# Second eight heads: products for the softmax maxima on half of the array's rows each, in pairs, with one maximum over two banks

## The chip, the core and the metric

The kernel runs on one core of a Trainium2 chip. The metric is the device time of one execution in microseconds (us). Engines are named as in the profile: PE is TensorE's matmul, PEld its loading of stationary operands ("weights"), DVE is VectorE, ACT ScalarE, POOL GpSimd, SP SyncE, which here only issues transfers (DMA).

## What is computed

One layer of attention with two kinds of heads, and one gated layer behind it. The change is in the attention of the second kind, `q_b`, `k_b`, `v_b`: eight query heads of width 64, four of which share one head of keys and values, 2048 queries, and 256 + 2048 keys.

```python
def block_attention(q, k, v, scale):
    ...
    def one_block(qi):
        sc = jnp.einsum('bqhgd,bthd->bhgqt', qi, k).astype(jnp.float32) * scale
        p = jax.nn.softmax(sc, axis=-1).astype(v.dtype)
        return jnp.einsum('bhgqt,bthe->bqhge', p, v)
    ...
o_a = block_attention(q_a[:, :, :, None], k_a, v_a, A_SCALE)        # 8 heads of width 96
o_b = block_attention(q_b.reshape(bsz, n, B_KV_HEADS, B_GROUP, B_HD), k_b, v_b, B_SCALE)   # 8 heads of width 64
```

Queries and keys are held as two fp32r numbers each, a rounded value (h) and the rest (l), so that a product of two such operands takes several matmuls.

## The kernel before, in words

`phase1` projects the input and leaves queries, keys and values in HBM. `attention` works through 64 **items**, one for each head and each quarter of the queries (512 of them): items 0 to 31 belong to the first eight heads, items 32 to 63 to the second. `phase3` is the output projection and the second layer.

An item has 18 **steps**, one for every 128 keys (`score`, then `low`, `add`, `mul`):

- `score`: PE makes the scores of 128 keys and 512 queries in PSUM (tile `s`, 3 buffers). In the second heads that is two matmuls: one over 128 rows (64 rows hold h, 64 rows l), and one over 65 rows, of which the last is a row of ones against the negative maximum of each query. ACT takes the exponential twice, once rounded (`ph`) and once in full, back into `s`.
- `low`: DVE subtracts the two and leaves `pl`. For two of the 18 steps POOL does this (the tuple `shares(i)[0]`), with a copy into `ph` first.
- `add`: POOL sums `ph` over the keys, for 12 of the 18 steps; for the other six PE adds them up with one matmul more (`ol<-ph,last`), and at the end with two (`sh`, `sl`).
- `mul`: four steps or more later PE multiplies `ph` and `pl` with the values (`oh`, `ol`).

The maxima must be there before an item's first score. Ten steps ahead (`AHEAD`) of it, and spread over 18 steps, `peak` has PE multiply queries and keys without their low halves into a tile `m` of one PSUM bank, two of which take turns (`peak_products`, L603 and L607), and `top` has DVE take the maximum over the keys (`peak_maxima`, L617 and L620): 16 times over 512 keys, and twice over 2 x 256 keys (two matmuls of 256 columns). At the last of them DVE takes the maximum of the 20 partial ones, negated (`nm`, L623), SP stores it to HBM (`NM<-nm`, L624), and `peak_row` loads it as a row of the query tile (`q<-NM`, L537), on which the 65-row matmul of the item's first step waits. [...]

The order on each of PE, DVE, ACT and POOL is written out: `at(time, unit)` gives each unit of work a time in steps, the units are sorted by it, and `InOrder` holds each engine to that order (its call is L588, hence one line for nearly all instructions of the attention). `queries` loads an item's query tile (3 buffers), `keys` the keys and values of a head (2 buffers); in the second heads a load of 64 rows each.

Of the kernel before, what the change touches and what calls it, by code (L numbers as in the profile page):

```python
# [12 lines left out]
F32 = mybir.dt.float32  # L13
F32R = mybir.dt.float32r
AF = mybir.ActivationFunctionType
ALU = mybir.AluOpType
AX = mybir.AxisListType
PSUM = bass.MemoryType.PSUM

P = 128  # L20
# [3 lines left out]
CTX = 256  # L24
NT = SEQ + CTX
NTT = NT // P
CH = 512
EPS = 1e-6
NH = 8
QR, KVR = 384, 256  # L30
NOPE, ROPE, DV = 64, 32, 64
HD = 64
# [36 lines left out]
def phase1(e):  # L69
    nc, tc, I = e.nc, e.tc, e.ins  # L70
    early = ExitStack()
    with tc.tile_pool(name="p1c", bufs=1) as cp, tc.tile_pool(name="p1", bufs=2, reuse_waits="tile") as sp, \
# [207 lines left out]
        for half in range(2):  # L280
# [197 lines left out]
            if half == 1:  # L478
                e.first = keys(e, 0), [queries(e, 0, g) for g in range(2)]
                todo = first_peaks(e, sp, pp)  # L480
# [55 lines left out]
def load(e, dst, src):  # L536
    e.nc.sync.dma_start(dst.bitcast(F32), src)  # L537


def keys(e, h):  # L540


    nc = e.nc
    K = e.kp.tile([P, 2, NT], F32R, name="k", tag="k", bufs=2)
    V = e.kp.tile([P, NTT, 2 * DV + 2], F32R, name="v", tag="v", bufs=2)
    if h < NH:
        load(e, K[:NOPE], e.KA[:, h * NOPE:(h + 1) * NOPE, :].rearrange("s p t -> p s t"))
        load(e, K[NOPE:NOPE + ROPE], e.KR.rearrange("s p t -> p s t"))
        nc.gpsimd.memset(K[NOPE + ROPE:NOPE + ROPE + 1, 0, :].bitcast(F32), 1.0)
        load(e, V[:, :, :2 * DV], e.VA[h])  # L550
    else:
        g = (h - NH) // 4
        load(e, K[:HD], e.KB[:, g * HD:(g + 1) * HD, :].rearrange("s p t -> p s t"))
        load(e, K[HD:, 0, :], e.KB[0, g * HD:(g + 1) * HD, :])
        nc.gpsimd.memset(K[HD:HD + 1, 1, :].bitcast(F32), 1.0)
        load(e, V[:, :, :2 * DV], e.VB[g])
    nc.gpsimd.memset(V[:, :, 2 * DV:2 * DV + 1].bitcast(F32), 1.0)
    return K, V


def queries(e, h, g):

    cs = slice(g * CH, (g + 1) * CH)
    Q = e.kp.tile([P, 2, CH], F32R, name="q", tag="q", bufs=3)
    if h < NH:
        load(e, Q[:NOPE], e.QN[:, h * NOPE:(h + 1) * NOPE, cs].rearrange("s p t -> p s t"))
        load(e, Q[NOPE:NOPE + ROPE], e.QP[:, h * ROPE:(h + 1) * ROPE, cs].rearrange("s p t -> p s t"))
    else:
        j = h - NH
        for i in range(2):  # L570
            load(e, Q[i * HD:(i + 1) * HD, 0, :], e.QB[i, j * HD:(j + 1) * HD, cs])
        load(e, Q[:HD, 1, :], e.QB[0, j * HD:(j + 1) * HD, cs])
    return Q


# [1 line left out]
AHEAD = 10  # L577
# [19 lines left out]
def peak_products(e, PE, pp, pms, at, i, K, Q, m, tag="m", bufs=2):  # L597

    r = NOPE + ROPE if at[0] < NH else P
    pm = pms[i, m] = pp.tile([P, CH], F32, name="m", tag=tag, bufs=bufs)  # L600
    if m < 16:
        j, c = divmod(m, 4)
        PE.matmul(pm, lhsT=Q[:r, 0, j * P:(j + 1) * P], rhs=K[:r, 0, c * CH:(c + 1) * CH], start=True, stop=True)  # L603
    else:
        for u in range(2):
            j = 2 * (m - 16) + u
            PE.matmul(pm[:, u * CTX:(u + 1) * CTX], lhsT=Q[:r, 0, j * P:(j + 1) * P], rhs=K[:r, 0, 4 * CH:],  # L607
                      start=True, stop=True)


def peak_maxima(e, DVE, sp, pms, stats, i, m):

    if m == 0:
        stats[i] = sp.tile([P, 4, 5], F32, name="mx", tag="mx", bufs=2)
    pm = pms.pop((i, m))
    if m < 16:
        DVE.tensor_reduce(out=stats[i][:, m // 4, m % 4:m % 4 + 1], in_=pm, axis=AX.X, op=ALU.max)  # L617
    else:
        j = 2 * (m - 16)
        DVE.tensor_reduce(out=stats[i][:, j:j + 2, 4], in_=pm.rearrange("p (j k) -> p j k", j=2), axis=AX.X, op=ALU.max)  # L620
    if m == 17:
        nm = sp.tile([P, 4], F32R, name="nm", tag="nm", bufs=2)
        DVE.tensor_reduce(out=nm, in_=stats.pop(i), axis=AX.X, op=ALU.max, negate=True)  # L623
        e.nc.sync.dma_start(e.NM[i:i + 1, :].rearrange("o (j p) -> p (o j)", p=P), nm.bitcast(F32))  # L624


def peak_row(e, h, i, Q):

    dst = Q[NOPE + ROPE:NOPE + ROPE + 1, 0, :] if h < NH else Q[HD:HD + 1, 1, :]
    load(e, dst, e.NM[i:i + 1, :])  # L630


def first_peaks(e, sp, pp):

    nc, (K, _), Q = e.nc, e.first[0], e.first[1]
    e.stats, pms = {}, {}

    def one(i, m):
        peak_products(e, nc.tensor, pp, pms, (0, i), i, K, Q[i], m, "misc", 3)
        peak_maxima(e, nc.vector, e.kp, pms, e.stats, i, m)  # L640

    return [lambda i=i, m=m: one(i, m) for i, n in ((0, NTT), (1, AHEAD)) for m in range(n)]


def attention(e):
# [3 lines left out]
    nc, tc = e.nc, e.tc  # L649
    PE, DVE, ACT, POOL = (InOrder(tc, x) for x in (nc.tensor, nc.vector, nc.scalar, nc.gpsimd))  # L650
# [3 lines left out]
    with tc.tile_pool(name="atc", bufs=1, reuse_waits="tile") as cp, \  # L654
            tc.tile_pool(name="at", bufs=2, reuse_waits="tile") as sp, \
            tc.tile_pool(name="atps", bufs=1, space=PSUM, reuse_waits="tile") as pp:
        NG = SEQ // CH
        work = [(h, g) for h in range(2 * NH) for g in range(NG)]
        NW = len(work)
        kv, qs, stats, pms, pts = {}, {}, {}, {}, {}  # L660
        acc, tot, gates, outs = {}, {}, {}, {}
        kv[0], (qs[0], qs[1]) = e.first

        last = cp.tile([P, DV + 2], F32R, name="last")
# [3 lines left out]
        def shares(i):  # L668

            if i >= NW - NG:  # L670
                return (), ()
            if i < NH * NG:
                return (4,), tuple(t for t in range(17) if t != 4)
            return (2, 8), tuple(t for t in range(16) if t not in (2, 5, 8, 12))

        def fetch_keys(h):
            kv[h] = keys(e, h) if h < NH or h % 4 == 0 else kv[h - 1]

        def fetch_queries(i):
            qs[i] = queries(e, *work[i])  # L680

        def peak(i, m):
            peak_products(e, PE, pp, pms, work[i], i, kv[work[i][0]][0], qs[i], m)

        def top(i, m):
            peak_maxima(e, DVE, sp, pms, stats, i, m)

        def row(i):
            peak_row(e, work[i][0], i, qs[i])

        def score(s):

            i, t = divmod(s, NTT)
            h, g = work[i]
            K, Q = kv[h][0], qs[i]
            ks = slice(t * P, (t + 1) * P)
            ps = pp.tile([P, CH], F32, name="s", tag="s", bufs=3)
            m = NOPE + ROPE
            if h < NH:
                prods = [(K[:m + 1, 0, ks], Q[:m + 1, 0, :]), (K[:m, 1, ks], Q[:m, 0, :]), (K[:m, 0, ks], Q[:m, 1, :])]  # L700
            else:
                prods = [(K[:, 0, ks], Q[:, 0, :]), (K[:HD + 1, 1, ks], Q[:HD + 1, 1, :])]
            for u, (a, b) in enumerate(prods):
                PE.matmul(ps, lhsT=a, rhs=b, start=u == 0, stop=u == len(prods) - 1)

            ph = sp.tile([P, CH], F32R, name="ph", tag="ph", bufs=LAGP + 3)
            pl = sp.tile([P, CH], F32R, name="pl", tag="pl", bufs=LAGP + 3)
            if t in shares(i)[0]:
                ps, pf = sp.tile([P, CH], F32, name="pf", tag="pf", bufs=2), ps
                ACT.activation(ps, pf, AF.Exp)  # L710
            else:
                ACT.activation(ph, ps, AF.Exp)
                ACT.activation(ps, ps, AF.Exp)
            pts[s] = (ph, pl, ps)
# [75 lines left out]
        def at(time, *unit):  # L790
            units.append((time, len(units), unit))

        stats.update(e.stats)
        for i in range(NW):
            if i > 1:
                at((i - 2) * NTT + 1.2, fetch_queries, i)
            if i % NG == 1 and i // NG + 1 < 2 * NH:
                at(i * NTT + 1.2, fetch_keys, i // NG + 1)
            for m in range((NTT, AHEAD)[i] if i < 2 else 0, NTT):
                at(i * NTT - NTT - AHEAD + m + 0.6, peak, i, m)  # L800
                at(i * NTT - NTT - AHEAD + m + 1.3, top, i, m)
            at(max(0, i * NTT - AHEAD + 2.5) - (i == 0), row, i)
        for s in range(NW * NTT):
            i, t = divmod(s, NTT)
            parts, adds = shares(i)
            at(s, score, s)
            at(s + (0.9 if t in parts else 1.6), low, s)
            if t in adds:
                at(s + 1.0, add, s)
            if adds and t == adds[-1]:  # L810
                at(s + 1.1, total, i)
            place = s + (LAGP if t in parts else LAG + (LATE[t] if t < len(LATE) else 0))
            at(place + 0.7, mul, s)
            if t == NTT - 1:
                at(place + 0.9, take, i)
                at(place + 2.3, finish, i)
# [16 lines left out]
            at(end - (NG - 1) * NTT + 4 * k + 17, lambda k: z_split(e, e.Z[0][k], sp.tile([P, CH], F32, name="zt", tag="zt", bufs=2), POOL), k)  # L833
        for _, _, (f, *args) in sorted(units):
            f(*args)


def phase3(e):
# [356 lines left out]
```

## Time and profile before

| | |
|---|---|
| time, median of 3 runs (range) | 3336.63 us (3332.5 to 3338.37) |
| the profiled execution: its own time, its span | 3341.19 us, 3339.4 us |
[...]
| PE, DVE, ACT, POOL busy, share of the span | 96%, 76%, 57%, 53% |
| scores of the first heads, and of the second | from 686.0 to 1536.34 us, and from there to 2319.4 us |

The attention is read from stretches of the span, not from the shares of the whole: in it DVE and POOL are far busier than the means say. A matmul's end is modelled, and a matmul of 512 columns is shown with 0.39 to 0.40 us although the next one starts 0.23 us later; so PE's pace is read from the starts of successive matmuls, and a wait from a start that comes late. The same holds for DVE, whose instructions overlap by some 0.08 us.

### The profile page before, as it was taken

To read this page: it belongs to the slowest core of one execution; us is meant where nothing else is said; L and a number is where in the kernel's file an instruction comes from. 1 tells how busy PE (TensorE), PEld (TensorE's weight loads), DVE (VectorE), ACT (ScalarE), POOL (GpSimd) and SP (SyncE) were. 2 spreads that over 40 slices of the span, in tenths; PEclk is the share of its full clock that TensorE was granted. 3 is DMA by queue.
4 is the path that set the end of the run, shared out by engine and by line. 5 is a ranking of instruction groups with operands and counts; after the bars stand their busy time and mean duration, and the time that the engine had idled before them with its cause. 6 is when DMAs were issued, how large, how long until landed. Compare 5 with 4: busy or idle time off the path is not lost.

```text
span 3339.4 us, 40476 instructions
## 1 busy us (share of the span) xinstructions
PE 3200.2 (96%) x13698; PEld 2435.2 (73%) x13698; DVE 2541.0 (76%) x3621; ACT 1890.9 (57%) x3258; POOL 1777.9 (53%) x1423
## 2 busy tenths in 40 slices
PE   7999999989999999999999999999899999899998
PEld 3886777767777777777666666677688788688786
DVE  4847794578988889888999999996745755755746
ACT  3433342257777777777777777776343353353342
POOL 3312431269999999998888888854301301301201
PEclk9999999989999999999999999999999999999999
DMA  6446745552122231222111111113533533533322
GB/s 231 141 163 188 231 146 188 159 124 62 39 49 60 60 65 39 49 60 60 30 28 30 28 43 33 28 29 61 158 94 108 151 95 110 146 97 108 107 89 76
DMA packets 187057, 314.09 MB, mean 94 GB/s; under 512 B 53264, under 2 KB 79184, under 8 KB 184928
## 3 DMA queue, kind: packets, MB, share of 16 engines
q1 hardware_dynamic: 178558, 283.62, 30.2%
q0 software_dynamic: 8000, 27.81, 2.8%
q8 instruction: 108, 1.77, 0.3%
q14 instruction: 101, 0.83, 0.1%
q10 hardware_dynamic: 290, 0.07, 0.0%
HBM read 240.71 MB, written 70.73 MB: 93 GB/s over the span
## 4 chain that ended last, share of the span: by engine, by line
PE 52%; DMA 10%; POOL 8%; DVE 8%; issue 5%; ACT 3%; SPq 0%; POOLq 0%; ACTq 0%; DVEq 0%
PE s L588 12%; POOL sa L588 6%; PE ol L588 6%; DMA NM<-nm 6%; PE oh L588 4%; PE m L588 4%; PE acc L1011 4%; PE acc L1010 4%; PE acc L1009 4%; PE acc L915 3%; PE acc L914 3%; PE acc L916 3%; DVE pl L588 2%; DMA q<-NM 2%; DMA w<-in_o_w_in 1%
## 5 line engine op out<-in xcount | busy, mean ns | idle before, releaser
L588 POOL TENSOR_TENSOR sa<-sa,ph 128x512 f32<-128x512 f32 x728 | 939.7, 1291 | 61.0 <-ACT ph L588 15.5
L588 PE MATMUL s<-q,k 96*128 96x512 f32 (+2 forms) x2880 | 874.3, 400 | 40.8 <-DVE pl L588 22.9
L588 DVE TENSOR_TENSOR pl<-s,ph 128x512 fp32r<-128x512 f32 x1064 | 728.6, 685 | 115.7 <-ACT s L588 93.0
L588 ACT ACTIVATE ph<-s 128x512 fp32r<-128x512 f32 x1064 | 633.7, 596 | 310.8 <-PE s L588 294.1
L588 DVE TENSOR_REDUCE mx<-m 128x1 f32<-128x512 f32 x1124 | 763.7, 682 | 58.7 <-PE m L588 55.2
L588 PEld LDWEIGHTS s<-q,k 96*128 96x128 f32 (+2 forms) x2880 | 538.9, 190 | 253.3 <-DVE pl L588 45.5
L588 ACT ACTIVATE s<-s 128x512 f32<-128x512 f32 x1064 | 632.7, 595 | 0.0
L588 PE MATMUL oh<-ph,v 128*128 128x512 f32 x1152 | 455.5, 395 | 0.0
L588 PE MATMUL ol<-pl,v 128*65 128x512 f32 x1152 | 455.1, 395 | 0.0
L588 PE MATMUL m<-k,q 128*128 128x512 f32 (+1 forms) x1250 | 451.2, 377 | 0.0
L65 ACT ACTIVATE wh<-w 128x1024 fp32r<-128x1024 f32 x153 | 162.2, 1060 | 491.3 <-PE acc L916 219.2
L66 DVE TENSOR_TENSOR wl<-w,wh 128x1024 fp32r<-128x1024 f32 x153 | 202.2, 1321 | 267.6 <-ACT wh L65 266.8
L1020 POOL TENSOR_TENSOR u<-u,y 128x512 f32<-128x512 f32 x32 | 63.6, 1988 | 416.7 <-ACT y L1019 416.7
L588 PEld LDWEIGHTS m<-k,q 128*128 128x128 f32 (+1 forms) x1250 | 234.7, 190 | 67.2 <-DVE mx L588 14.3
L177 PE MATMUL ps<-xl,wh 128*128 128x512 f32 (+1 forms) x640 | 250.3, 391 | 6.9 <-DVE xl L168 6.8
L176 PE MATMUL ps<-xh,wh 128*128 128x512 f32 (+1 forms) x640 | 249.1, 390 | 6.3 <-POOL wh L147 3.4
L588 PEld LDWEIGHTS oh<-ph,v 128*128 128x128 f32 x1152 | 217.9, 189 | 49.5
L178 PE MATMUL ps<-xh,wl 128*128 128x512 f32 (+1 forms) x640 | 248.8, 389 | 1.7 <-DVE wl L148 1.7
L588 PEld LDWEIGHTS ol<-pl,v 128*65 128x65 f32 x1152 | 157.4, 137 | 50.7 <-ACT ob L588 0.3
L914 PE MATMUL acc<-wh,k 128*128 128x512 f32 x384 | 159.7, 416 | 24.1 <-DVE y L1046 18.6
L915 PE MATMUL acc<-wl,k 128*128 128x512 f32 x384 | 158.4, 412 | 8.5 <-DVE wl L66 8.4
L916 PE MATMUL acc<-wh,k 128*128 128x512 f32 x384 | 156.9, 409 | 0.0
(300 smaller groups left out, 5372.5 us busy)
## 6 DMA issues: line engine op xcount, KB each, us to landing
w<-in_wug SPq DMA_DIRECT2D x64, 512.0 KB
wr<-in_w SPq DMA_DIRECT2D x38, 512.0 KB
w<-in_e_w_out SPq DMA_DIRECT2D x32, 512.0 KB
w<-in_o_w_in SPq DMA_DIRECT2D x32, 512.0 KB
w<-in_o_w_out SPq DMA_DIRECT2D x32, 512.0 KB
wr<-in_e_w_mod SPq DMA_DIRECT2D x24, 512.0 KB
wr<-in_o_w_mod SPq DMA_DIRECT2D x24, 512.0 KB
q<-QB SPq DMA_DIRECT2D x96, 128.0 KB
```

Of the source, the lines that this page charges most:

```text
L65: e.nc.scalar.activation(h, src, AF.Copy)
L66: e.nc.vector.tensor_tensor(out=l, in0=src, in1=h.bitcast(F32), op=ALU.subtract)
L176: nc.tensor.matmul(out, lhsT=wh(k), rhs=xh(k), start=i == 0, stop=False)
L177: nc.tensor.matmul(out, lhsT=wh(k), rhs=xl(k), start=False, stop=False)
L178: nc.tensor.matmul(out, lhsT=wl(k), rhs=xh(k), start=False, stop=i == n - 1)
L588: i = getattr(self.engine, name)(*args, **kw)
L914: nc.tensor.matmul(ps[t], lhsT=h[:, ts], rhs=w[0][:, k, :], start=first, stop=False)
L915: nc.tensor.matmul(ps[t], lhsT=h[:, ts], rhs=w[1][:, k, :], start=False, stop=False)
L916: nc.tensor.matmul(ps[t], lhsT=l[:, ts], rhs=w[0][:, k, :], start=False, stop=last)
L1009: nc.tensor.matmul(ps, lhsT=w[0][:, k, :], rhs=h, start=k == 0, stop=False)
L1010: nc.tensor.matmul(ps, lhsT=w[0][:, k, :], rhs=l, start=False, stop=False)
L1011: nc.tensor.matmul(ps, lhsT=w[1][:, k, :], rhs=h, start=False, stop=k == NK - 1)
```

## The change

For the second heads alone, products for the maxima are made in pairs. The keys' high halves, which lay in rows 0 to 63 of the key tile, now lie there and in rows 64 to 127, and so do the queries'. A product contracts over 64 rows; one of a pair uses rows 0 to 63, the next one rows 64 to 127, and they write two neighbouring banks of one tile `m` of two banks, of which there is one buffer (before: two buffers of one bank). The pair is made at every second step. One maximum instruction takes both banks: 8 with 2 x 512 keys, and one with 4 x 256. The pool of `m` is closed and opened anew at item 32, where the form of the tile changes.

The scores' second matmul has 128 rows in place of 65: rows 0 to 63 are now ones in row 0 against the negative maximum, and zeros, which POOL sets once for each head of keys. A query tile is loaded with four transfers of 64 rows in place of three. The first heads, the scores themselves, exponentials, sums and products with the values are as before.

```diff
@@ keys @@
     else:
         g = (h - NH) // 4
-        load(e, K[:HD], e.KB[:, g * HD:(g + 1) * HD, :].rearrange("s p t -> p s t"))
-        load(e, K[HD:, 0, :], e.KB[0, g * HD:(g + 1) * HD, :])
-        nc.gpsimd.memset(K[HD:HD + 1, 1, :].bitcast(F32), 1.0)
+        load(e, K[HD:], e.KB[:, g * HD:(g + 1) * HD, :].rearrange("s p t -> p s t"))
+        load(e, K[:HD, 0, :], e.KB[0, g * HD:(g + 1) * HD, :])
+        nc.gpsimd.memset(K[:HD, 1, :].bitcast(F32), 0.0)
+        nc.gpsimd.memset(K[:1, 1, :].bitcast(F32), 1.0)
         load(e, V[:, :, :2 * DV], e.VB[g])
@@ queries @@
         for i in range(2):
             load(e, Q[i * HD:(i + 1) * HD, 0, :], e.QB[i, j * HD:(j + 1) * HD, cs])
-        load(e, Q[:HD, 1, :], e.QB[0, j * HD:(j + 1) * HD, cs])
+
+        for i in range(2):
+            load(e, Q[i * HD:(i + 1) * HD, 1, :], e.QB[0, j * HD:(j + 1) * HD, cs])
@@ new @@
+def pair_products(PE, pm, K, Q, m):
+
+    parts = [(Q[:HD, 0], K[:HD, 0]), (Q[HD:, 1], K[HD:, 0])]
+    for u in range(1 if m < 8 else 2):
+        for v, (q, k) in enumerate(parts):
+            if m < 8:
+                j, c = divmod(2 * m + v, 4)
+                PE.matmul(pm[:, v], lhsT=q[:, j * P:(j + 1) * P], rhs=k[:, c * CH:(c + 1) * CH], start=True, stop=True)
+            else:
+                j = 2 * v + u
+                PE.matmul(pm[:, v, u * CTX:(u + 1) * CTX], lhsT=q[:, j * P:(j + 1) * P], rhs=k[:, 4 * CH:], start=True, stop=True)
+
+
+def pair_maxima(e, DVE, sp, pm, stats, i, m):
+
+    if m == 0:
+        stats[i] = sp.tile([P, 4, 5], F32, name="mx", tag="mx", bufs=2)
+    if m < 8:
+        j, c = divmod(2 * m, 4)
+        DVE.tensor_reduce(out=stats[i][:, j, c:c + 2], in_=pm, axis=AX.X, op=ALU.max)
+    else:
+        DVE.tensor_reduce(out=stats[i][:, :, 4], in_=pm.rearrange("p v (u k) -> p (v u) k", u=2), axis=AX.X, op=ALU.max)
+        stored(e, DVE, sp, stats, i)
@@ peak_row @@
-    dst = Q[NOPE + ROPE:NOPE + ROPE + 1, 0, :] if h < NH else Q[HD:HD + 1, 1, :]
+    dst = Q[NOPE + ROPE:NOPE + ROPE + 1, 0, :] if h < NH else Q[:1, 1, :]
@@ attention @@
         def peak(i, m):
-            peak_products(e, PE, pp, pms, work[i], i, kv[work[i][0]][0], qs[i], m)
+            if i < NH * NG:
+                peak_products(e, PE, mp[0], pms, work[i], i, kv[work[i][0]][0], qs[i], m)
+            elif m % 2:
+                pms[i] = mp[0].tile([P, 2, CH], F32, name="m", tag="m", bufs=1)
+                pair_products(PE, pms[i], kv[work[i][0]][0], qs[i], m // 2)
 
         def top(i, m):
-            peak_maxima(e, DVE, sp, pms, stats, i, m)
+            if i < NH * NG:
+                peak_maxima(e, DVE, sp, pms, stats, i, m)
+            elif m % 2:
+                pair_maxima(e, DVE, sp, pms.pop(i), stats, i, m // 2)
...
-                prods = [(K[:, 0, ks], Q[:, 0, :]), (K[:HD + 1, 1, ks], Q[:HD + 1, 1, :])]
+                prods = [(K[:, 0, ks], Q[:, 0, :]), (K[:, 1, ks], Q[:, 1, :])]
```

`stored` holds the three lines that made `nm` and its store, word for word; they follow the ninth maximum now.

PE in the steady part of the second heads, before: in a row of four steps or so, where `s` are the scores, `m` the products for the maxima, `oh` and `ol` those with the values.

```order
L588 MATMUL m<-k,q 128x512
L588 MATMUL oh<-ph,v 128x512
L588 MATMUL ol<-pl,v 65x512
L588 MATMUL s<-q,k 128x512 x2
L588 MATMUL m<-k,q 128x512
L588 MATMUL oh<-ph,v 128x512
L588 MATMUL ol<-pl,v 65x512
```

The same place after the change:

```order
L591 MATMUL m<-k,q 128x512 x2
L591 MATMUL oh<-ph,v 128x512
L591 MATMUL ol<-pl,v 65x512
L591 MATMUL s<-q,k 128x512 x2
L591 MATMUL oh<-ph,v 128x512
L591 MATMUL ol<-pl,v 65x512
L591 MATMUL s<-q,k 128x512 x2
L591 MATMUL m<-k,q 128x512 x2
```

Two products `m` stand side by side at every second step where one stood at each; the full-height matmuls between two such places are six (or seven, with an `ol<-ph,last`).

DVE in the same part, before: maxima (`mx`) and subtractions (`pl`) alternate, and `nm` closes an item's maxima.

```order
L588 TENSOR_REDUCE mx<-m 128x2
L588 TENSOR_TENSOR pl<-s,ph 128x512
L588 TENSOR_REDUCE mx<-m 128x2
L588 TENSOR_REDUCE nm<-mx 128x4
L588 TENSOR_TENSOR pl<-s,ph 128x512
L588 TENSOR_REDUCE mx<-m 128x1 x2
L588 TENSOR_TENSOR pl<-s,ph 128x512
L588 TENSOR_REDUCE mx<-m 128x1
L588 TENSOR_TENSOR pl<-s,ph 128x512
```

The same place after the change:

```order
L591 TENSOR_TENSOR pl<-s,ph 128x512 x2
L591 TENSOR_REDUCE mx<-m 128x4
L591 TENSOR_REDUCE nm<-mx 128x4
L591 TENSOR_TENSOR pl<-s,ph 128x512
L591 TENSOR_REDUCE mx<-m 128x2
L591 TENSOR_TENSOR pl<-s,ph 128x512 x2
L591 TENSOR_REDUCE mx<-m 128x2
L591 TENSOR_TENSOR pl<-s,ph 128x512 x2
```

A maximum now stands between two pairs of subtractions, and `nm` follows a single maximum of four columns instead of two of two.

## Rows read from the trace of the kernel before

**Rows 1.** Busy time by stretch: length, PE, PEld, DVE, ACT, POOL, PEclk, DMA, GB/s.
```profile
1497.00:1523.00 26.00, 26.00 (x115) 20.08 (x114) 23.38 (x39) 19.90 (x37) 23.70 (x20) 1.00 0.10 25
1601.00:2211.00 610.00, 593.44 (x2502) 420.99 (x2503) 565.16 (x928) 479.75 (x900) 509.83 (x426) 1.00 0.13 31
```
**Rows 2.** Timeline of SP's issues: start, us, engine, line, operation, tiles.
```profile
1601.32 0.39 SPq L624 DMA_DIRECT2D NM<-nm  x1
...
1992.18 0.39 SPq L624 DMA_DIRECT2D NM<-nm  x1
2000.91 0.22 SPq L537 DMA_DIRECT2D q<-NM  x1
2003.20 1.73 SPq L537 DMA_DIRECT2D q<-QB  x3
```
**Rows 3.** Timeline of PE, a run of eight matmuls without a wait, second heads.
```profile
2021.98 0.39 PE L588 MATMUL m<-k,q 128*128 128x512 f32 x1
...
2023.85 0.62 PE L588 MATMUL s<-q,k 128*128 128x512 f32 x2
```
**Rows 4.** Timeline of PE where it waits; in brackets, idle time and what ended it.
```profile
2004.43 0.50 PE L588 MATMUL s<-q,k 65*128 65x512 f32 x1 [0.32 <-DMA q<-NM]
...
2012.22 0.40 PE L588 MATMUL m<-k,q 128*128 128x256 f32 x2
2012.46 0.39 PE L588 MATMUL oh<-ph,v 128*128 128x512 f32 x1
2012.69 0.40 PE L588 MATMUL ol<-pl,v 128*65 128x512 f32 x1
2013.56 0.73 PE L588 MATMUL s<-q,k 128*128 128x512 f32 x2 [0.48 <-DVE pl L588]
2014.16 0.51 PE L588 MATMUL m<-k,q 128*128 128x256 f32 x2
2014.51 0.39 PE L588 MATMUL oh<-ph,v 128*128 128x512 f32 x1
```
**Rows 5.** Groups of 1601 to 2211 us: count, busy us, mean ns, idle before.
```profile
L588 DVE TENSOR_REDUCE mx<-m 128x1 f32<-128x512 f32 (+1 forms) x451 | 305.4, 682 | 21.9 <-PE m L588 21.2
L588 PE MATMUL s<-q,k 128*128 128x512 f32 (+1 forms) x902 | 294.7, 404 | 16.6 <-DVE pl L588 12.3 <-DMA q<-NM 3.4
```
**Rows 6.** Timeline of DVE, second heads, without a wait.
```profile
2011.38 1.40 DVE L588 TENSOR_TENSOR ob<-oh,ob 64x512 f32<-64x512 f32 x2
...
2016.53 0.17 DVE L588 TENSOR_REDUCE nm<-mx 128x4 fp32r<-128x20 f32 x1
...
2017.22 1.28 DVE L588 TENSOR_REDUCE mx<-m 128x1 f32<-128x512 f32 x2
```
**Rows 7.** Timeline of POOL at the same place.
```profile
2016.71 0.62 POOL L588 TENSOR_SCALAR ph<-pf 128x512 fp32r<-128x512 f32 x1
...
2018.66 4.03 POOL L588 TENSOR_TENSOR sa<-sa,ph 128x512 f32<-128x512 f32 x3
```
**Rows 8.** Timeline of PE where matmuls of 2 columns (L118, L273) meet full ones.
```profile
17.79 7.03 PE L118 MATMUL ps<-wr,sc 128*2 128x512 f32 x16
...
534.91 0.39 PE L178 MATMUL ps<-xh,wl 128*128 128x512 f32 x1
535.23 3.59 PE L273 MATMUL rows<-acc,pick 128*2 128x512 f32 x8
538.75 0.51 PE L176 MATMUL ps<-wh,ch 128*128 128x512 f32 x1
539.10 0.40 PE L177 MATMUL ps<-wl,ch 128*128 128x512 f32 x1
```
**Rows 9.** Timeline of PE where matmuls of 64 columns (L418) meet full ones.
```profile
556.97 0.39 PE L418 MATMUL ps<-xl,wh 128*64 128x512 f32 x1
557.20 0.39 PE L176 MATMUL ps<-xh,wh 128*128 128x512 f32 x1
557.42 0.39 PE L177 MATMUL ps<-xl,wh 128*128 128x512 f32 x1
```

More of the change, by code (lines that the diff above doesn't have):

```diff
@@ L608, in peak_products, with stored @@
                       start=True, stop=True)
+def pair_products(PE, pm, K, Q, m):
[17 more added lines that the diff above has]
+        stored(e, DVE, sp, stats, i)
+def stored(e, DVE, sp, stats, i):
+    nm = sp.tile([P, 4], F32R, name="nm", tag="nm", bufs=2)
+    DVE.tensor_reduce(out=nm, in_=stats.pop(i), axis=AX.X, op=ALU.max, negate=True)
+    e.nc.sync.dma_start(e.NM[i:i + 1, :].rearrange("o (j p) -> p (o j)", p=P), nm.bitcast(F32))
 def peak_maxima(e, DVE, sp, pms, stats, i, m):
@@ L621, in peak_maxima @@
     if m == 17:
-        nm = sp.tile([P, 4], F32R, name="nm", tag="nm", bufs=2)
-        DVE.tensor_reduce(out=nm, in_=stats.pop(i), axis=AX.X, op=ALU.max, negate=True)
-        e.nc.sync.dma_start(e.NM[i:i + 1, :].rearrange("o (j p) -> p (o j)", p=P), nm.bitcast(F32))
+        stored(e, DVE, sp, stats, i)
 def peak_row(e, h, i, Q):
-    dst = Q[NOPE + ROPE:NOPE + ROPE + 1, 0, :] if h < NH else Q[HD:HD + 1, 1, :]
+    dst = Q[NOPE + ROPE:NOPE + ROPE + 1, 0, :] if h < NH else Q[:1, 1, :]
     load(e, dst, e.NM[i:i + 1, :])
@@ L661, in attention, with banks @@
         acc, tot, gates, outs = {}, {}, {}, {}
+        mpool, mp = ExitStack(), []
+        def banks(k):
+            mpool.close()
+            mp[:] = [mpool.enter_context(tc.tile_pool(name="mps%d" % k, bufs=1, space=PSUM, reuse_waits="tile"))]
+        banks(0)
         kv[0], (qs[0], qs[1]) = e.first
@@ L798, in attention @@
                 at(i * NTT + 1.2, fetch_keys, i // NG + 1)
+            if i == NH * NG:
+                at(i * NTT - NTT - AHEAD + 0.6, banks, 1)
             for m in range((NTT, AHEAD)[i] if i < 2 else 0, NTT):
@@ L835, in attention @@
             f(*args)
+        mpool.close()
 def phase3(e):
```

## The prediction

> **What bounds the kernel now.** I first ask which engine sets the pace of the second heads, since only there anything changes. The length of an item comes from SP's issues: the store of the maxima `NM<-nm` returns once per item, and from 1601.32 to 1992.18 us it returns 16 times [rows 2], so an item takes 24.43 us. What PE needs for it comes from a run without a wait: from 2021.98 to 2023.85 us eight matmuls start, one every 0.234 us [rows 3]. By the code an item has 36 of them for scores, 18 + 18 with the values, 8 that sum `ph`, and 16 of 512 columns plus 4 of 256 for the maxima. That is 96 x 0.234 = 22.5 us, and the four short ones take 0.24 us for one pair (2012.22 to 2012.46) and 0.35 for the other (2014.16 to 2014.51) [rows 4]: 23.1 us together. So PE is occupied for 23.1 of 24.43 us and waits for about 1.4 us per item. The reader sees where: at the first step for the row of maxima (`q<-NM`, 0.32 us), some nine microseconds later for `pl` (0.48 us) [rows 4], in sum 12.3 us for `pl` and 3.4 for the row over 25 items [rows 5]; the rest is small change around these.
>
> The other engines are close behind. DVE starts an instruction of 512 columns every 0.60 us (two in 1.28 us, the last 0.68 long) [rows 5, 6]; 16 subtractions and 18 maxima are 20.4 us, two `ob` 1.4 and `nm` 0.1: 21.9 us. POOL has 15 operations at 4.03 / 3 = 1.34 us and two copies of 0.62 [rows 7]: 21.3 us. In the first heads, where PE's need is larger (three matmuls per score), it has no gap at all, 26.00 busy of 26.00 us, with DVE and POOL at 90% [rows 1]. So whatever PE gains in the second heads meets POOL and DVE after some two microseconds, and whatever it loses is paid almost in full, less the part of the 1.4 us of waits that goes away.
>
> **The change, part by part.**
>
> *Maxima on DVE.* 682 ns for 512 columns and 174 for the 20 of `nm` [rows 5, 6] give 1.03 ns per column, so 1024 columns end 0.53 us later: 1.13 us from start to start. Nine of them are 10.2 us against 18 x 0.60 = 10.8. DVE needs 21.3 us instead of 21.9, a saving of 0.6 us on an engine that isn't the bound; it can only shorten the waits for `pl`. Against this stands that `nm` comes 0.53 us later behind its last product.
>
> *Products side by side.* Two products took 0.468 us of PE's stream. If both halves of the array run at once, a pair takes 0.234. No row of before shows two matmuls at once; the bounds are 0.234 and 0.468. I take 0.234: the two share no row of the array and no PSUM bank, and PE does overlap what shares nothing (in [rows 3] each matmul's weights are loaded under the one before, or eight could not start every 0.234 us). [...]
>
> *Going to the half array and back.* This is the term that decides. The trace has a place where PE leaves the full array for a small part of it and returns: eight matmuls with 2 columns of weights among full ones [rows 8]. Sixteen such matmuls take 7.03 us and eight take 3.59, so one takes 0.43. The first one starts 0.32 us after the full matmul in front, not 0.234: 0.09 us to go there. Eight take 3.52 us to the start of the next full one, not 3.44: 0.08 to 0.09 back. And the second full one starts 0.35 us after the first, not 0.234: 0.11, since its predecessor's weights weren't loaded ahead. The other such place speaks against a price: matmuls with 64 columns of weights pass into full ones at 0.23 and 0.22 us [rows 9]. Which of the two is the pair like? Those with 2 columns leave most of the array unused as the halves do, and run in fp32; those with 64 columns are fp32r, as the products here are. I go by [rows 8], since the halves have to run side by side to be of use, so the array really must be divided, and nothing in [rows 9] gains from a division. [...]
>
> The pair is then 0.09 in + 0.11 for weights that can't be loaded ahead + 0.234 for both + 0.09 out + 0.11 for the next full weights = 0.63 us, and 0.74 if the second half's weights queue behind the first's. Against 0.468 that is +0.17 to +0.28; I take +0.22, eight times per item: +1.8. The ninth group, four matmuls of 256 columns, took 0.59 and takes 0.09 + 0.11 + two rounds of 0.12 + 0.09 + 0.11 = 0.64, up to 0.97 with three more unhidden loads: +0.05 to +0.4, taken as +0.2. PE's need rises by 2.0 us per item (1.4 to 2.6), to 25.1.
>
> *What comes back.* With 25.1 us of its own PE runs against DVE's and POOL's 21.3, nearly the relation of the first heads, where it waits for nothing. The wait for `pl` stands behind the two `ob` (1.40 us of DVE at once [rows 6]) and should halve, as the step grows longer and DVE's share of it shorter. The wait for `q<-NM` stays: from the store's issue at 1992.18 to the first score that uses it at 2004.43 is 12.25 us [rows 2, 4]; `nm` comes 0.53 us later, and ten steps of PE's longer pace give about as much back. I take 0.5 us off the 1.4 (0.1 to 1.0).
>
> *The rest.* The fourth load of queries adds an issue of 1.73 / 3 = 0.58 us on SP [rows 2], behind `q<-NM` and seven steps ahead of its use; queued behind it is the store of the previous item, for which nobody waits. The second matmul of a score has 128 rows in place of 65 and the same 512 columns, which set its time: nothing. Zeros on POOL: twice in all. The single tile `m` of two banks makes PE wait for the maximum two steps (2.7 us) earlier; 0.4 + 1.13 us and a subtraction of 0.60 in front fit. Where the `ob` fall in between, 1.4 us more don't quite: up to 0.5 us per item, inside my upper bound.
>
> Sum: +2.0 - 0.5 = +1.5 us per item, for 32 items +48 us (0.4 to 2.5 per item: +13 to +80). On the profiled execution's 3341.19 us that is 3389; it lies 4.6 us above the median of the runs, so the forecast for the median is 3385 (3350 to 3417).
>
> **Rivals.**
>
> *The change to half the array is free*, as in [rows 9]. Then PE saves 8 x 0.234 + 0.3 = 2.2 us and needs 20.9, and POOL's and DVE's 21.3 become the bound. But the ring over HBM also stands: 12.25 us from store to score, plus 0.53, plus the 11.6 us from there to the next store (24.43 - 12.25, less some 0.6 of waits), now at 21.3 / 23.1 of their length: 23.5 us. So 0.9 us less per item at the least, 2.5 at the most (21.3 and a wait of 0.6); taken as 1.2, -38 us: 3299 (3257 to 3308). It decides as soon as both crossings and their loads cost under 0.234 us together. For it: [rows 9], the same number type. Against: [rows 8]. [...]
>
> *The two halves run one after the other*, so the change doesn't do what it says. A pair is 0.09 + 0.11 + 0.468 + 0.09 + 0.11 = 0.87 us, +0.40; with +0.4 for the ninth group +3.6 per item. Waits give back 0.8: +2.8, +90 us, 3427 (3405 to 3455). Speaking for it: no row shows an overlap of matmuls.
>
> *Waits swallow the price.* Crossings fall where PE would have waited for DVE anyway and nearly all of the 1.4 us goes away: +0.0 to +0.2 per item, 3330 to 3343. Against it: pairs stand at fixed steps, waits at two or three of 18.
>
> **How the numbers follow.** Forecast 0.55, one after the other 0.17, free 0.20, swallowed 0.08. The likeliest is 3385. The range takes in all but the free case and the far end of the serial one: 3330 to 3440. A measurement of this kernel tells about 0.2% (7 us) from no change; so slower 0.72, same 0.07 and faster 0.21, which is the free case and the swallowed one's edge.
>
> **What would show it.** In the profile after: the item's length from the `NM<-nm` issues, 25.9 us if right, 23.2 if the change is free, 27.2 if serial. Around a pair on PE, from the last full matmul's start to the first full one's after the pair: 0.76 to 0.87 us in place of 0.70 (0.47 if free, 0.99 if serial), the two products' starts at most 0.11 apart, and the second full matmul behind a pair 0.34 us after the first. Weight loads behind a pair that start with their matmul, not ahead. Maxima of 1.2 us. I am wrong if the pair's products start 0.23 apart, or if full weights are loaded while a pair runs.

## The result, and the profile after

The change made the kernel slower: 3358.7 us (3356.24 to 3361.63) against 3337.5 us for the kernel before, a ratio of 1.0063 [1.0045, 1.0082]. The forecast was 3385 with a range of 3330 to 3440: the direction and the range hold, but the loss is 21 us where 48 were forecast.

The busy times from the head of the profile page of after, and its chain of work that ended last. PE was the longest part of that chain in before too, with 52% (last line here, from the page of before); it now has 64%, and the transfers (DMA) have fallen from 10% to 4%.

```profile
PE 3223.2 (96%) x13698; PEld 2363.2 (70%) x13698; DVE 2523.4 (75%) x3333; ACT 1894.4 (56%) x3258; POOL 1777.1 (53%) x1425
PE 64%; DVE 8%; DMA 4%; ACT 4%; issue 4%; POOL 3%; POOLq 0%; SPq 0%; ACTq 0%; DVEq 0%
```
```profile
PE 52%; DMA 10%; POOL 8%; DVE 8%; issue 5%; ACT 3%; SPq 0%; POOLq 0%; ACTq 0%; DVEq 0%
```

The busy time of the same stretch as in [rows 1], with the same columns. PE gained 4.7 us of busy time, though 24.4 items fall into the stretch and not 25.0; DVE lost 26. The granted clock is 1.00 in both (over the whole span it is 0.984 in before and 0.986 in after), so the clock has no part in this.

```profile
1601.00:2211.00 610.00, 598.11 (x2441) 358.07 (x2442) 538.83 (x685) 469.51 (x877) 498.00 (x417) 1.00 0.14 35
```

The issues of SP in after, which answer to [rows 2] (start, us, engine, line, operation, tiles). The store of the maxima now returns every 25.00 us, and keeps to that within 0.04. In before it returned after 24.43 on average of the rows; over the 22 items that all item lengths below are taken from (the middle of the second heads) it is 24.40, with single items from 23.7 to 24.8.

```profile
2003.90 0.39 SPq L642 DMA_DIRECT2D NM<-nm  x1
2014.80 0.22 SPq L537 DMA_DIRECT2D q<-NM  x1
...
2028.90 0.39 SPq L642 DMA_DIRECT2D NM<-nm  x1
...
2053.90 0.39 SPq L642 DMA_DIRECT2D NM<-nm  x1
```

PE of after around the ninth group and a pair (same columns; in brackets idle time and what ended it), which answers to [rows 3, 4].

```profile
2000.26 0.74 PE L591 MATMUL s<-q,k 128*128 128x512 f32 x2
2001.39 0.51 PE L591 MATMUL m<-k,q 64*128 64x256 f32 x4 [0.39 <-DVE mx L591]
2001.83 0.49 PE L591 MATMUL oh<-ph,v 128*128 128x512 f32 x1
2002.16 0.39 PE L591 MATMUL ol<-pl,v 128*65 128x512 f32 x1
...
2003.32 0.62 PE L591 MATMUL s<-q,k 128*128 128x512 f32 x2
2003.87 0.50 PE L591 MATMUL m<-k,q 64*128 64x512 f32 x2
2004.30 0.50 PE L591 MATMUL oh<-ph,v 128*128 128x512 f32 x1
2004.64 0.39 PE L591 MATMUL ol<-pl,v 128*65 128x512 f32 x1
2004.87 0.39 PE L591 MATMUL ol<-ph,last 128*65 128x512 f32 x1
```

Read the starts. Two full scores start at 2003.32; the second of them starts 0.23 later, at 2003.55, and the pair 0.32 after that, not 0.234: the way into the half array costs 0.09. The next full matmul starts 0.43 after the pair and the one behind it 0.34 later, before the pace of 0.23 returns. The two products of the pair end together after 0.50 us; the trace's records have their starts 3 ns apart. So the stretch from the last full start to the second full start is 0.326 + 0.425 + 0.338 = 1.09 us, where before it was four matmuls, 4 x 0.234 = 0.94. **One pair costs 0.155 us more than the two full products that it replaces.** At the seven steps where a pair follows without a wait the mean over the 22 items lies between 0.152 and 0.159. What the array does in the 0.09 us on the way in, no row shows.

The weight loads of the same stretch say where the rest goes. Both halves' weights load in one time of 0.19 us, and they start with the pair (2003.87), not under the matmul ahead. The next full weights start with their own matmul (2004.30). Full weights among full matmuls are loaded ahead: those of the scores that start at 2004.87 + 0.23 start at 2004.87.

```profile
2003.09 0.42 PEld L591 LDWEIGHTS s<-q,k 128*128 128x128 f32 x2
2003.87 0.19 PEld L591 LDWEIGHTS m<-k,q 64*128 64x128 f32 x2 [0.36 <-DVE nm L591]
2004.30 0.19 PEld L591 LDWEIGHTS oh<-ph,v 128*128 128x128 f32 x1 [0.24 <-issue]
...
2004.87 0.42 PEld L591 LDWEIGHTS s<-q,k 128*128 128x128 f32 x2
```

The groups of 1650 to 2200 us (count; busy us, mean ns; idle before). The wide maximum takes 1220 ns. The scores, which waited 16.6 us in [rows 5], wait for nothing that the view names; the products for the maxima now wait, and for the maximum ahead of them.

```profile
L591 PE MATMUL s<-q,k 128*128 128x512 f32 x792 | 243.3, 397 | 0.0
L591 DVE TENSOR_REDUCE mx<-m 128x2 f32<-128x1024 f32 (+1 forms) x198 | 241.6, 1220 | 26.2 <-PE m L591 26.2
L591 PE MATMUL m<-k,q 64*128 64x512 f32 (+1 forms) x440 | 99.0, 463 | 10.7 <-DVE mx L591 8.7
```

The waits of PE between 1625 and 2162 us (total us, times, longest), first of before, then of after: two waits have gone and a new one has come, once per item.

```profile
PE s L588 <- DVE pl L588: 10.8, 22, 0.5
PE s L588 <- DMA q<-NM: 3.2, 10, 0.5
```
```profile
PE m L591 <- DVE mx L591: 8.8, 22, 0.4
```

The chain of waits of after, from 1996.4 us on (start, us, what), shows how the new wait comes about. ACT copies the finished sums (`ob`), so its next `ph`, `s` and `ph` come late; then `pl`, then the maximum on DVE, and only when that has read the single tile `m` may PE write the ninth group into it.

```profile
1997.45 0.59 ACT ob L591
1998.04 0.48 ACT ph L591
1998.53 0.48 ACT s L591
1999.01 0.52 ACT ph L591
1999.53 0.67 DVE pl L591
2000.21 1.14 DVE mx L591
...
2001.39 0.51 PE m L591 x4
```

DVE's own rows of the same microseconds end at the same point: its two `ob` run to 1999.48, so `pl` could not have started earlier even with its input there.

```profile
1998.07 1.41 DVE L591 TENSOR_TENSOR ob<-oh,ob 64x512 f32<-64x512 f32 x2 [0.16 <-ACT ob L591]
1999.51 0.69 DVE L591 TENSOR_TENSOR pl<-s,ph 128x512 fp32r<-128x512 f32 x1
2000.12 1.21 DVE L591 TENSOR_REDUCE mx<-m 128x2 f32<-128x1024 f32 x1
2001.25 1.28 DVE L591 TENSOR_TENSOR pl<-s,ph 128x512 fp32r<-128x512 f32 x2
```

The sum for an item, from these rows: PE needed 23.05 and needs 23.05 + 8 x 0.155 + 0.04 (ninth group) = 24.33. The item went from 24.40 to 25.00, so the time that PE stands still or starts late went from 1.35 to 0.67. Of the price of 1.28 only 0.60 was paid, and 32 items at 0.60 are 19 of the 21 us.

### The profile page after: what moved, and what is told of

Its sections match the earlier page's. It is cut to its first block, busy times and chain, and to the rows that moved or that the text cites. A ratio compares the mean times of both kernels' runs of the same rounds, so it can differ in the third digit from the quotient of the medians.

```text
span 3354.4 us, 40220 instructions
## 1 busy us (share of the span) xinstructions
PE 3223.2 (96%) x13698; PEld 2363.2 (70%) x13698; DVE 2523.4 (75%) x3333; ACT 1894.4 (56%) x3258; POOL 1777.1 (53%) x1425
## 4 chain that ended last, share of the span: by engine, by line
PE 64%; DVE 8%; DMA 4%; ACT 4%; issue 4%; POOL 3%; POOLq 0%; SPq 0%; ACTq 0%; DVEq 0%
PE s L591 15%; PE ol L591 9%; PE oh L591 8%; PE m L591 6%; PE acc L1061 4%; PE acc L1060 4%; PE acc L1059 4%; PE acc L964 3%; PE acc L965 3%; PE acc L966 3%; DVE mx L591 2%; POOL sa L591 2%; DMA NM<-nm 2%; DVE pl L591 2%; PE ps L176 1%
## 5 line engine op out<-in xcount | busy, mean ns | idle before, releaser
L591 PE MATMUL s<-q,k 96*128 96x512 f32 (+2 forms) x2880 | 854.9, 398 | 23.7 <-DMA q<-NM 15.7
L591 DVE TENSOR_REDUCE mx<-m 128x1 f32<-128x512 f32 (+3 forms) x836 | 725.5, 868 | 69.5 <-PE m L591 66.8
L591 PE MATMUL oh<-ph,v 128*128 128x512 f32 x1152 | 485.1, 421 | 0.0
L591 PE MATMUL m<-k,q 64*128 64x512 f32 (+1 forms) x1250 | 362.3, 420 | 13.7 <-DVE mx L591 11.1
L591 PEld LDWEIGHTS m<-k,q 64*128 64x128 f32 (+1 forms) x1250 | 172.6, 186 | 152.6 <-DVE mx L591 50.6
L964 PE MATMUL acc<-wh,k 128*128 128x512 f32 x384 | 157.4, 410 | 21.2 <-DVE y L1096 18.6
L147 POOL TENSOR_SCALAR wh<-wr 128x1024 fp32r<-128x1024 f32 (+1 forms) x48 | 56.1, 1170 | 187.7 <-PE ps L177 103.3
```

Source lines behind the costliest of these rows:

```text
L591: i = getattr(self.engine, name)(*args, **kw)
L964: nc.tensor.matmul(ps[t], lhsT=h[:, ts], rhs=w[0][:, k, :], start=first, stop=False)
```

## Experiments

**What the parts of the change do.** Four kernels, run on one chip beside the kernel before (3325.09 us there).

Without the half array; the pairs, the two-bank tile and the wide maximum stay:

```diff
-    parts = [(Q[:HD, 0], K[:HD, 0]), (Q[HD:, 1], K[HD:, 0])]
+    parts = [(Q[:, 0], K[:, 0])] * 2
```


> The changed kernel with both products of a pair over all 128 rows, as before the change; pairs, the tile of two banks and the one maximum stay. PE never goes to half the array, so its own need is back at 23.1 us per item, DVE's need is the changed kernel's 21.3. Theory A (waits shrank because PE's own need grew; the wide maximum has little part in it): waits are back near 1.4 us, item 24.2 to 24.5 us, time 3331 to 3341. Rival B (waits shrank because DVE does less): waits stay near 0.7 us, item about 23.7, time about 3314.

Measured: 3334.23 us, 1.0028 [1.0017, 1.0039], item 24.26. The saving on DVE (0.6 us per item) brought nothing; the kernel still lost a little against before on this chip, since PE waits here for the maximum in front of the ninth group as it does in after. Its waits between 1625 and 2162 us:

```profile
PE m L591 <- DVE mx L591: 9.2, 23, 0.4
```

So the tile of two banks, of which there is one, makes a wait of its own, without any half array. The starts of PE show more of it than this view, which leaves out idle times under 0.15 us: the products `m` start late, against the pace of 0.234, by 0.56 us at the ninth group and by 0.09 and 0.22 at two other steps, 0.86 per item together. The scores behind `pl` are late by 0.23 us per item here and by 0.77 in a before of the same speed (the trace of the next experiment).

Two maxima of 512 in place of the wide one, the rest as in after:

```diff
-        DVE.tensor_reduce(out=stats[i][:, j, c:c + 2], in_=pm, axis=AX.X, op=ALU.max)
+        for v in range(2):
+            DVE.tensor_reduce(out=stats[i][:, j, c + v:c + v + 1], in_=pm[:, v], axis=AX.X, op=ALU.max)
```
(The ninth group likewise.)

> The changed kernel with two maxima of 512 columns in the place of each one of 1024; products on half the array as changed. DVE's need is back at 21.9 us per item. Theory A: PE's need of 24.3 us still sets the pace, item 25.0 to 25.2, time 3358 to 3366. Rival B: waits are back at 1.4, item 25.7, time about 3381.

Measured: 3359.73 us, 1.0106 [1.0089, 1.0124], item 25.14. The wide maximum is worth 0.13 us per item in after: real, but a fifth of what it saves on DVE.

Both products on the same half of the array, which should rule out that they run side by side:

```diff
-    parts = [(Q[:HD, 0], K[:HD, 0]), (Q[HD:, 1], K[HD:, 0])]
+    parts = [(Q[:HD, 0], K[:HD, 0])] * 2
```


> The changed kernel with both products of a pair in rows 0 to 63, so that they can't run side by side; as many crossings, the same DVE work. If the two really run at once in the changed kernel, a pair costs 0.21 to 0.23 us more, PE's need is 26.2 to 26.4 us per item, waits 0.2 to 0.7: item 26.4 to 27.0, time 3404 to 3423. If they ran one after the other there too, nothing changes: 25.0 and 3359.

Measured: 3406.3 us, 1.0247 [1.0232, 1.0262], item 26.68, that is 1.68 more than after, 0.21 for each of eight pairs. PE's timeline of this kernel shows a pair that takes 0.67 us to the next full matmul, where in after it took 0.43; the two products are busy 0.73, not 0.50:

```profile
2002.13 0.73 PE L591 MATMUL m<-k,q 64*128 64x512 f32 x2
2002.80 0.50 PE L591 MATMUL oh<-ph,v 128*128 128x512 f32 x1
```

So in after the halves do run side by side; that the change does what it says is shown, and the rival "one after the other" is out.

Before, with six of the sixteen products of an item done twice, which adds 6 x 0.234 = 1.4 us to PE's need and changes nothing else:

```diff
-        PE.matmul(pm, lhsT=Q[:r, 0, j * P:(j + 1) * P], rhs=K[:r, 0, c * CH:(c + 1) * CH], start=True, stop=True)
+        for _ in range(2 if at[0] >= NH and m % 3 == 0 else 1):
+            PE.matmul(pm, lhsT=Q[:r, 0, j * P:(j + 1) * P], rhs=K[:r, 0, c * CH:(c + 1) * CH], start=True, stop=True)
```


> The kernel before the change, with six of the 16 full-height products per item of the second heads made twice into the same bank: 6 x 0.234 = 1.4 us more for PE, no crossing, DVE as before. Theory A: PE's need of 24.45 takes waits away as in the changed kernel, item 25.0 to 25.3, time 3356 to 3366. Rival B: waits stay 1.4, item 25.8, time about 3382.

Measured: 3350.34 us, 1.0079 [1.0062, 1.0096], item 24.87. Of 1.4 us only 0.87 was paid against the 24.00 of before at this speed (the next experiment has that number; the 25.0 to 25.3 expected had started from 24.40). The wait for `pl` fell to half, as the prediction had it for the change:

```profile
PE s L588 <- DVE pl L588: 5.5, 21, 0.3
```

So the waits shrink because PE needs longer, with DVE's work untouched. The other account, that the smaller work on DVE takes the waits away, has the run without the half array against it, where DVE's work is smaller and the item is not shorter.

**Why the kernel before is not everywhere the same.** On this chip before took 3325 us, where the first comparison had 3337.5. Both kernels were run again unchanged, on another chip.

> The kernel before, unchanged, on the chip of the runs beside it, for a trace to compare with theirs. Item 24.4 us and ratio 1.000 if its pace is the same on every chip. Rival: on the chips where the others stood 9 to 11 us further from it than their items account for, its own item is shorter (24.1 us), with shorter waits for the row of maxima from HBM.

> The changed kernel, unchanged, on the same chip as the kernel before. Item 25.0 us, ratio 1.006 if the distance is the same on every chip; 1.009 to 1.010 if the kernel before alone gains on this one.

Measured: before 3322.45 us (0.9996 [0.9987, 1.0005] against itself), after 3355.48, 1.0097 [1.0082, 1.0113]. The item of after is 25.01 as on the first chip; that of before is 24.00, not 24.40. So the rival named ahead held: before alone gains on this chip. Its waits between 1625 and 2162 us lack one line of the earlier list, the wait for `q<-NM`, and in its chain of work that ended last the transfers have 2% where the first trace of before had 10%:

```profile
PE s L588 <- DVE pl L588: 10.6, 22, 0.5
```
```profile
PE 55%; POOL 12%; DVE 6%; ACT 6%; issue 5%; DMA 2%; POOLq 0%; SPq 0%; ACTq 0%; DVEq 0%
```

From the store's issue to the row's issue it is 8.36 us here (median of 22 items), 8.67 in the first trace of before. The starts of PE say where the 0.40 us lie. In the first trace the second score of an item's first step, which uses the row, starts 0.33 us late on average, and the product behind it 0.08; here both start on time, and PE's other late starts differ by 0.01 us at most. So the kernel before stands at the edge of the way of its maxima over HBM (store `NM<-nm`, then load `q<-NM`): some tenths of a microsecond more there cost it 0.4 us per item. After stands clear of that edge, so the ratio between the two depends on the chip: it was 1.0036 to 1.0097 in four comparisons. On this chip the loss is 1.00 us per item, and it divides: 24.26 - 24.00 = 0.26 for the pairs with one tile and the wide maximum, 25.00 - 24.26 = 0.74 for the half array. (The run without the half array was on the chip with 3325.09; its before has no trace, and I take the 24.00 of the one with 3324.94.) The spans of these two traces differ by 33.1 us, of which 22.1 lie in the 22 items, 7.5 in the six items at the change from the first heads to the second, 5.5 in the last five, and -2.0 in the rest.

**Can the new wait be taken away?** Theory: the two `ob` (1.4 us of DVE) stand in front of the maximum that frees the tile; if they come one step later, the wait goes and the item falls to PE's need. Once in after, once in the kernel without the half array:

```diff
-                at(place + 2.3, finish, i)
+                at(place + (2.3 if i < NH * NG or i >= NW - NG else 3.4), finish, i)
```


> The changed kernel with the two sums ob of an item's end (DVE, 1.4 us together) 1.1 steps later in the second heads, behind the last maximum but one and not ahead of it. Theory: PE's remaining wait for the maximum ahead of the ninth group (0.39 us idle, 0.46 with the late start) is due to the ob in front of that maximum on DVE and goes away: item 24.5 to 24.7 us, 10 to 16 us less than the changed kernel. Rival: it comes back as a wait for pl at the next scores: item 24.9 to 25.1, no change.

> The kernel with pairs and wide maxima but products over all 128 rows (item 24.26), with the same move of the two ob. Theory: its waits of 0.56 us for the maximum and some of those for pl go away: item 23.6 to 23.8, 10 to 20 us below the kernel before. Rival: the wait comes back for pl: item 24.2 to 24.3, within 0.3% of the kernel before.

Measured: 3376.65 us, 1.0166 [1.0147, 1.0185], item 25.88; and 3362.03 us, 1.012 [1.0101, 1.014], item 25.39. Both are slower by 0.9 and 1.1 us per item. The wait for `mx` shrank, as meant, and a larger one for `pl` came in its place. In the first of the two:

```profile
PE s L591 <- DVE pl L591: 18.4, 21, 0.9
PE m L591 <- DVE mx L591: 3.3, 21, 0.2
```

The theory fell. Its rival, that the wait comes back for `pl`, had the mechanism but not the size: it expected no change (24.9 to 25.1 and 24.2 to 24.3).

A second try was to let PE reach the ninth group later:

```diff
-                at(i * NTT - NTT - AHEAD + m + 0.6, peak, i, m)
+                at(i * NTT - NTT - AHEAD + m + (0.95 if i >= NH * NG and m == 17 else 0.6), peak, i, m)
```


> The changed kernel with the ninth group of products (four of 256 columns) 0.35 steps later, on PE behind that step's products with the values and no longer ahead of them. Theory: PE's wait for the maximum in front of that group (0.46 us with the late start) is covered by two or three matmuls that don't depend on it: item 24.5 to 24.7 us, 10 to 16 us below the changed kernel. Rival: it comes back elsewhere, at the next scores: item 24.9 to 25.1.

> Pairs and wide maxima with products over all 128 rows (item 24.26), and the same later ninth group. Theory: item 23.7 to 23.9 us against 24.0 of the kernel before on these chips, ratio 0.996 to 1.000. Rival: the wait moves, item 24.2 to 24.3, ratio 1.003.

Measured: 3363.61 us, 1.0036 [1.0023, 1.0049], item 25.01; and 3346.46 us, 0.9984 [0.9975, 0.9994], item 24.45. These tell nothing of the theory: no other work of the list has a due time between 0.6 and 0.95 of that step, so the edit left the order of instructions as it was. They are repeats of after and of the kernel without the half array, on one more chip, where before takes 3351.16 us. As such they are of use. After's item is the same there. The kernel without the half array, 24.26 on the other chip, waits for the row here and is 0.19 longer, with 9.11 us from the store's issue to the row's where it was 8.53. Most of these waits leave too little idle time to be in the line below; by the starts of PE the score with the row is 0.12 us late on average and the product behind it 0.08, which is the 0.19. Against before of its chip this kernel is slower at 1.0028 there and a little faster at 0.9984 here.

```profile
PE s L591 <- DMA q<-NM: 0.4, 2, 0.2
```

Why before takes 3351 us on this chip stays open, as there is no trace of it from there. A part can lie in the first heads, which wait for their row too: in after's repeat their stretch from the 4th to the 31st store takes 716.2 us here and 711.0 on the chip with 3324.94, and PE's waits for `q<-NM` between 674 and 1472 us add up to 15.9 and 9.5 us.

The price of the half array by itself was measured in the kernel before, with its products singly on rows 0 to 63 (18 visits to the half array per item):

```diff
-    r = NOPE + ROPE if at[0] < NH else P
+    r = NOPE + ROPE if at[0] < NH else HD
```


> The kernel before, with the products for the maxima of the second heads over rows 0 to 63 alone, one at every step as before: 18 crossings to half the array and back per item instead of 9, nothing side by side. If a crossing and its return cost what they do in the changed kernel, a product takes 0.09 + 0.425 + 0.10 us in place of 0.234 (+0.39) and a group of two short ones 0.2 to 0.25 more: +6.7 us per item for PE, which then waits for little: item 29.5 to 30.0, time about 180 us above before (ratio 1.050 to 1.058). Rival: returning at once is cheaper than after a pair, or part is hidden: item under 28.5.

Measured: 3515.76 us, 1.049 [1.0469, 1.051], item 29.86. PE's timeline of this kernel, one product between full matmuls:

```profile
2002.60 0.63 PE L588 MATMUL s<-q,k 128*128 128x512 f32 x2
2003.16 0.50 PE L588 MATMUL m<-k,q 64*128 64x512 f32 x1
2003.59 0.50 PE L588 MATMUL oh<-ph,v 128*128 128x512 f32 x1
2003.92 0.40 PE L588 MATMUL ol<-ph,last 128*65 128x512 f32 x1
```

It is the pattern of after, 0.33, 0.43 and 0.33 from start to start, for one product instead of two. So a visit to the half array costs 0.33 + 0.43 + 0.34 - 3 x 0.234 = 0.39 us beside its own product, whether one or two products run there. The item agrees: 29.86 less the former need of 23.05 is 6.8 us, 0.38 for each of 18 visits, and PE waits for nothing that the view names. A pair saves one product, 0.234, and pays 0.39: the 0.155 of above.

**One step more ahead.** The maxima are computed AHEAD = 10 steps before the place where the item that uses them starts. One step more moves the ninth group against the `ob`, and gives the way over HBM a step more. Three kernels, beside after once more, on another chip (before 3338.93 us):

```diff
-AHEAD = 10
+AHEAD = 11
```


> The changed kernel, unchanged, beside the next three on one chip. Item 25.0 us whatever the chip; ratio between 1.004 and 1.010, by how long the way of the maxima over HBM takes for the kernel before on this chip.

> The changed kernel with the maxima one step further ahead (AHEAD 11 in place of 10), so that the two ob come right behind a pair's maximum on DVE and not right in front of one. Theory: the 0.46 us that PE waits in front of the ninth group goes away and nothing takes its place: item 24.4 to 24.6 us, 13 to 19 us below the changed kernel of the same chip. Rival: the wait moves to the scores (pl), item 24.9 to 25.2.

> Pairs and wide maxima, products over all 128 rows, AHEAD 11. Theory: item 23.6 to 23.9 us whatever the chip, 5 to 25 us below the kernel before. Rival: 24.2 and no gain, as the wait moves.

> The kernel before with AHEAD 11 and nothing else: 1.3 us more for the way of the maxima over HBM. If chips differ by that way alone, the item is 24.0 here whatever the chip, and the kernel is 0 (fast way) to 12 us (slow way) below the kernel before. Rival: the item differs by chip all the same, 24.4 on a slow one.

| kernel | us | ratio | item |
|---|---|---|---|
| after, unchanged | 3358.71 | 1.0062 [1.0047, 1.0078] | 25.01 |
| after, 11 ahead | 3377.51 | 1.0112 [1.0095, 1.0129] | 25.53 |
| without the half array, 11 ahead | 3360.55 | 1.0063 [1.0048, 1.0078] | 25.05 |
| before, 11 ahead | 3323.8 | 0.9952 [0.9938, 0.9967] | 23.99 |

Both kernels with the wide maximum missed what was expected, the rival's range too (25.2 and 24.2 at most). In after the wait for `mx` is all but gone (0.2 us in all) and again one for `pl` has come, 0.67 in place of 0.39. DVE's rows and then PE's of that kernel: the two `ob` run to 1989.55, and the `pl` for which PE waits stands behind them.

```profile
1988.15 1.40 DVE L591 TENSOR_TENSOR ob<-oh,ob 64x512 f32<-64x512 f32 x2
1989.59 1.29 DVE L591 TENSOR_TENSOR pl<-s,ph 128x512 fp32r<-128x512 f32 x2
```
```profile
1988.49 0.51 PE L591 MATMUL m<-k,q 64*128 64x256 f32 x4
...
1990.33 0.73 PE L591 MATMUL s<-q,k 128*128 128x512 f32 x2 [0.67 <-DVE pl L591]
```

So PE's wait came back for `pl`, and grew, in all four kernels that moved the block of 1.4 us or the maxima beside it. Whether splitting it helps wasn't tried.

In before the step more is a gain: on a chip where the unchanged kernel takes 3338.93 us its item is 23.99, as on the chip where the maxima came early, and no wait for `q<-NM` is left in the list, though the store-to-row time is 8.59 us, nearly that of the first trace:

```profile
PE s L588 <- DVE pl L588: 10.4, 22, 0.5
```

On this chip this version is faster than both kernels, than before by 15.1 us or 0.5% (0 to 12 us were expected). The score with the row starts on time in all 22 items, and PE's other late starts add up to what they were in the faster trace of before (1.06 against 1.07 us per item), although the step moves other instructions too. So it is the late row that costs before its 0.4 us per item where it is slower. The unchanged kernel has no trace from this chip, and the version wasn't run on a chip where before is fast; nothing says that it gains there.

## Why the forecast was right in sign and wrong in size

- **What bounds the kernel** was read rightly: PE's need sets the pace of the second heads, and what PE loses is paid, less some of the waits. Six products done twice show it without any half array: 0.87 of 1.4 us.
- **The maxima on DVE**: 1.13 us from start to start was worked out for the wide one, and the rows have it (2000.12 to 2001.25, with 1.22 long). That the saving can't help much was right too: it is worth 0.13 us per item.
- **Side by side**: taken as 0.234 for both, and so it is; the two runs on one half show what the other case would have cost.
- **Crossing** was taken from the matmuls with 2 columns [rows 8], against those with 64 columns [rows 9], which show no price. That choice was right: 0.09 us into the half array, and full weights that aren't loaded ahead. The rival of a free change is out.
- **The mis-sized terms**, which are the step that failed: the sum for an item was +2.0 - 0.5 = +1.5 us and measured +1.28 - 0.68 = +0.60. Of the 0.90 too much, 0.56 is the price of the pairs, 0.16 the ninth group and 0.18 what comes back. First, a pair was priced at +0.17 to +0.28 and taken in the middle, +0.22, since the second half's weights might queue behind the first's. They don't: both load at once, and the pair costs +0.155, just under the lower bound. Eight pairs: 1.24 in place of 1.8. Second, the ninth group was taken as +0.2, with loads that queue again; it measured +0.04, its lower bound (+0.05). Together PE's need rose by 1.28, not by 2.0.
- **What comes back**: taken as 0.5 us, measured 0.68 on the first chip (waits from 1.35 to 0.67) and 0.28 on the chip with the faster before (from 0.95). The forecast of this term was for the kernel as traced, and there it was 0.2 short. That it came so near is luck, as each wait went another way than forecast. The wait for `q<-NM` was said to stay; it is gone, and with it 0.41 us of late starts per item. The longer item gives the row of maxima more time (from the store's issue to the item's first score it is 12.46 us in after and 11.54 in before, medians): on the chip where before takes 3351 us, with 9.1 us from store to row in both, the kernel with items of 24.45 waits for the row and after with 25.01 doesn't. The wait for `pl` was to halve; it fell to almost nothing.
- **The rest** held a new wait as an upper bound only: PE in front of the ninth group where the `ob` fall in between, "up to 0.5 us". It is there in each item, with 0.39 idle and a start 0.46 late, and a smaller one of 0.16 at another step. It should have been in the sum. Its cost is part of the 0.26 us by which the kernel without the half array is longer than the faster before.
- The signs that were named ahead came out as follows: item 25.0 (25.9 forecast; 23.2 if free, 27.2 if one after the other); last full start to first full start behind a pair 0.75 (0.76 to 0.87); next full one 0.34 later, as forecast; the two products' starts 3 ns apart (at most 0.11).

## What to carry to other kernels

Matmuls on half of the array's rows had a price per visit here, not per product: 0.39 us in front of a gain of 0.234 for each product that runs beside another, so two products per visit lose. By this sum, which is an estimate, the visits must be made fewer, with more products in each, before the division pays; no run here had more than one pair of full width in a visit. On an engine that isn't the bound, fewer and wider instructions on one larger buffer can cost more than they save, since the buffer's reader now holds up its writer (without the half array 24.26 against 24.00 us per item here, with 0.6 us less for DVE to do; on the chip where before takes 3351 us the ratio was 0.9984). And before two versions are compared on several chips, look for a transfer that arrives just in time: one step of slack for it was worth 0.5% where it was tried, nearly as much as the whole change cost there (0.6%).

## What the runs showed of the hardware

- The visit to the half array: 0.326 us from the last full start to the pair, 0.425 back to the first full one, 0.338 to the second, where the full array runs at 0.234; the same for one product as for two.
- Weights of the two halves load at the same time (two in 0.19 us, where one takes 186 ns on average), but not under the full matmul ahead of them: they start with the pair, 0.32 us behind that matmul's start. Full weights don't load under the pair either: they start with their own matmul, 0.43 us behind the pair's.
- One maximum over 1024 columns in two banks takes 1.22 us, 1.13 from start to start, against 2 x 0.60 for two of 512.
- The way of 2 KB from a store's issue to the issue of the load behind it took 8.3 to 9.1 us (medians over the 22 items of each trace), and the same kernel differed from one set of runs to the next: after 8.40, 8.88, 8.95 and 9.09 in four, three of them on chips known to be different.
